# Lower halves of one gate-up chunk in eight: from a POOL transfer instead of VectorE

## The chip, the cores and the metric

One core of a Trainium2 chip runs the kernel. The metric is the time of one execution on the device in microseconds; the median of several runs is given.

## The reference

One layer of a hybrid encoder on 256 tokens with 2048 features, in float32. Two of its parts are feed-forward networks (FFN), one at the start and one at the end, with 5632 inner features:

```
def swiglu(x, w_gate_up, w_down):
    gate, up = jnp.split(x @ w_gate_up, 2, axis=-1)
    return (jax.nn.silu(gate) * up) @ w_down

ff = swiglu(rms_norm(x, pre_norm_ffn1), w_ffn1_gate_up, w_ffn1_down)
x = x + 0.5 * rms_norm(ff, post_norm_ffn1)
...  # one combined projection, HGRN2 recurrence, windowed attention, output projection
ff = swiglu(rms_norm(x, pre_norm_ffn2), w_ffn2_gate_up, w_ffn2_down)
x = x + 0.5 * rms_norm(ff, post_norm_ffn2)
```

The change is in `x @ w_gate_up`, a product of 256 x 2048 by 2048 x 11264, in both FFNs.

## The kernel before

**Numbers in two parts.** TensorE multiplies a shorter float type (`F32R`). To keep float32's accuracy each operand is taken as an upper part `h`, its rounding to that type, and a lower part `l`, the remainder `x - h`, and a product is three: `ah*h`, `ah*l`, `al*h` (`three`, each of its matmuls is on line 415). The weights are split on the way. Each half chunk of 128 x 1024 weights comes into `raw`, ScalarE copies it into `h` with the rounding (line 175), and VectorE subtracts, `l = raw - h` (line 176). `split_half` makes the two tiles, `split` and `split_load` do so for both halves of a chunk.

**Gate-up.** `Gated` works in `NG` = 11 groups (`group(g)`, g from 0 to 10), each of 512 gate columns with the 512 up columns that belong to them. A group goes over the 2048 input features in eight chunks of 256 (`order`, `work`, `pos` from 0 to 7). A chunk is 1 MB of weights, loaded in two transfers of 512 KB on SP's queue (`load`, line 151), one for each half, and one half (index k) is 128 features by 512 gate and 512 up columns. An ordinary chunk is 24 matmuls: 2 halves x 2 blocks of 128 tokens x 2 column blocks x 3, the first half's twelve ahead of the second's, and in each three the second uses `l`. The chunks at positions 2 and 4 (`sums`, `seven`) are done with seven block products instead of eight, 21 matmuls, and need four splits and some sums on VectorE first. At position 6 the seven products are folded into the four banks (`fold`, lines 477 to 485), and there, as at position 5, the products go bank by bank. After a group, `units` makes silu(gate) * up (ScalarE line 844, VectorE line 845), transposes it on TensorE (line 856) and splits it into `ht`. A group's transposes run after the next group's chunk 0.

**Buffers.** `raw` has three buffers (`rawp`, 1 MB each), `h` and `l` have five each (`hip`, `lop`, a half chunk each). A new tile waits for the last reader of the tile it takes the place of: a copy into `h` for TensorE's products on the `h` five before, a load into `raw` for the last engine that read the `raw` three before.

**Order.** Each engine runs its instructions in the order of its own list, and waits at each for the semaphores that it needs. For this part the order within an engine follows the program, moved about a little by the planner that places the instructions; it is written out by hand only at the start and at the seams between stages (`manual_schedule`). POOL's queue is used for small vectors at the start (line 116 and lines 995 to 1006), and POOL itself for a few small operations.

Of the kernel before, what the change touches and what calls it, by code (L numbers as in the profile page):

```python
# [11 lines left out]
F32 = mybir.dt.float32  # L12
F32R = mybir.dt.float32r
# [4 lines left out]
ALU = mybir.AluOpType  # L18
AX = mybir.AxisListType

P = 128
# [16 lines left out]
def hymba_layer_kernel(  # L38
# [25 lines left out]
    nc = tc.nc  # L64
# [4 lines left out]
    hip = ctx.enter_context(tc.tile_pool(name="hip", bufs=5))  # L69
    lop = ctx.enter_context(tc.tile_pool(name="lop", bufs=5))  # L70
# [5 lines left out]
    def nm(s):  # L76
        uid[0] += 1
        return f"{s}_{uid[0]}"
# [61 lines left out]
    def load(src, between=None):  # L140
        raw = rawp.tile([P, 2048], F32, tag="raw", name=nm("raw"))
        if len(src.shape) == 4:

            dst = raw.rearrange("p (a n b) -> p a n b", a=src.shape[1], n=src.shape[2])
            parts = [(dst[:, a], src[:, a]) for a in range(src.shape[1])]
        else:
            parts = [(raw.rearrange("p (a b) -> p a b", a=src.shape[1]), src)]
        for i, (to, of) in enumerate(parts):
            if i and between:
                between()  # L150
            nc.sync.dma_start(to, of)
        return raw

    def split_load(src, hp=hip, lp=lop, between=None, middle=None):
        return split(load(src, between), hp, lp, middle)

    def split(raw, hp=hip, lp=lop, middle=None):
        hs, ls = [], []
        for i in range(2):
            if i and middle:  # L160
                middle()
            h, l = split_half(raw, i, hp, lp)
            hs.append(h)
            ls.append(l)
        return hs, ls

    def split_half(raw, i, hp=hip, lp=lop):
        part = raw[:, i * 1024 : (i + 1) * 1024]
        h = hp.tile([P, 1024], F32R, tag="h", name=nm("h"))
        l = lp.tile([P, 1024], F32R, tag="l", name=nm("l"))  # L170
        split_act(h, l, part)
        return h, l

    def split_act(hi, lo, src):
        nc.scalar.copy(hi, src)  # L175
        nc.vector.tensor_tensor(lo, src, hi.bitcast(F32), ALU.subtract)  # L176
# [144 lines left out]
    class LeadN:  # L321


        def __init__(self, w, c0, slot):
            self.w, self.c0, self.slot = w, c0, slot
# [56 lines left out]
    class Blocks:  # L382
# [3 lines left out]

        def __init__(self, tiles, sums):
            self.tiles, self.sums = tiles, sums

        def begin(self, order, c=None):  # L390

            self.order, self.pos, self.seen = order, 0, {}
            self.c = c or [[pa(), pa()], [pb(), pb()]]
            self.p = None
            at = [i for i, u in enumerate(order) if u in self.sums]
            some = len(at)
            plain = len(order) - some
            self.after = at[-1] + 1 if at else len(order) - 1

            self.rest = 6 * (len(order) - self.after - 1)  # L400
            self.of = {}
            for i in range(4):
                self.of["p", i] = 3 * some
                self.of["c", i // 2, i % 2] = 6 * plain + (3 * some if i < 3 else 0)
# [25 lines left out]
        def seven(self, u):  # L430
# [9 lines left out]
                four[:, 0:2], four[:, 0::3], four[:, 1:2].to_broadcast([P, 2, 512]), ALU.add  # L440
            )
            lower = split_half(raw, 1)
            nc.vector.tensor_tensor(b22, b11, b22, ALU.add)  # L443
            upper = split_half(raw, 0)
            nc.vector.tensor_tensor(b21, b22, b21, ALU.add)  # L445
            last = split_half(raw, 1)
# [40 lines left out]
        def work(self, upto):  # L487

            while self.pos < upto:
                u = self.order[self.pos]  # L490
                if u in self.sums:
                    self.seven(u)
                else:
                    hs, ls = split_load(self.source(u))
                    if self.pos == self.after + 1:
                        self.fold()
                    places = [(k, m, n) for k in range(2) for m in range(2) for n in range(2)]
                    if self.pos in (self.after, self.after + 1):

                        places.sort(key=lambda at: at[1:])  # L500
                    for k, m, n in places:
                        self.plain(u, hs, ls, m, n, k)
                self.pos += 1
# [253 lines left out]
    class Gated(Blocks):  # L757
# [6 lines left out]

        def group(self, g, c=None):
            self.g = g
            self.begin(range(KT // 2), c)

        def source(self, u):
# [27 lines left out]
    def ffn(gated, w_dn, post_gain, again, gain=None, lead=None, aside=None):  # L797

        with ExitStack() as st:
# [96 lines left out]

            again_order = [u for u in order if u < NU - LATE] + [u for u in order if u >= NU - LATE]
            rows = Pairs(w_dn, [order, again_order], hts, sums, work, post_gain)
            rows.half_gain(far["pool"])
            rows.work(1)  # L900
# [16 lines left out]
    with tc.manual_schedule():  # L917
# [9 lines left out]
        raw = rawp.tile([P, 2048], F32, tag="raw", name=nm("raw"))  # L927
        first = gated.source(0)

        def arrive(i):  # L930
            nc.sync.dma_start(raw[:, i * 512 : (i + 1) * 512], first[:, i // 2, i % 2])

        h, l = (
            p.tile([P, 1024], F32R, tag=t, name=nm(t)) for p, t in ((hip, "h"), (lop, "l"))
        )
# [32 lines left out]
        hs, ls = zip((h, l), split_half(raw, 1))  # L968
# [519 lines left out]
```

## Time and profile before

| | |
|---|---|
| median of 3 runs | 1866.79 us (1866.19 to 1867.09) |
| the profiled execution | 1864.63 us |
| its span | 1862.9 us |
| granted TensorE clock | 0.999 |
| TensorE, VectorE, ScalarE, POOL busy | 1842.0, 1539.1, 1070.6, 33.7 us |
| DMA | 365.79 MB, mean 196 GB/s |
| first FFN's groups 1 to 10 | about 62 to 492 us, 43.06 us each |
| second FFN's groups 1 to 10 | about 1192 to 1622 us |

In the rows, PE is TensorE, PEld its weight loads, DVE is VectorE, ACT is ScalarE, POOL is GpSimd, SP issues transfers; a name with q is that engine's queue or sequencer. A row of the timeline has start, length (us), engine, line, operation, tile written <- tiles read, shape, and in brackets the idle time of the engine ahead of it with what ended it. A row of groups has count, busy time, mean length in ns, then idle time and its releasers. A busy TensorE counts its matmuls with their modelled ends, each 0.39 us long though one starts every 0.227 us.

### The profile page before, as it was taken

Reading aid. Unit: us, or ns where it says so; the run is one execution under the profiler, and the core shown is the slowest. Engines: PE = TensorE matmul, PEld = TensorE weight load, DVE = VectorE, ACT = ScalarE, POOL = GpSimd, SP = SyncE. Lnnn points to the kernel's source line nnn. Section 1 sums busy time; section 2 is a strip of 40 time slices with the busy share of each in tenths; the row PEclk is TensorE's granted clock in tenths of the full one; section 3 lists DMA queues with packets and bytes.
Section 4 is the critical chain, followed back from the end, with each engine's and each line's share of the span. In section 5 each row is a group of like instructions: output and inputs, shape, how many; then the busy total and the mean of one; then the engine's idle time right before and its main releaser. Section 6 shows DMA issues by size and latency. Waiting matters only on the chain.

```text
span 1862.9 us, 23299 instructions
## 1 busy us (share of the span) xinstructions
PE 1842.0 (99%) x8680; PEld 1534.1 (82%) x8680; DVE 1539.1 (83%) x1924; ACT 1070.6 (57%) x1429; POOL 33.7 (2%) x47
## 2 busy tenths in 40 slices
PE   8999999999999999999999999999999999999998
PEld 6888888888887887888888887888888888887886
DVE  6988888888888888567787788988888788888887
ACT  6555555555555556576677656555555555565553
POOL 1000000000000002000000001000000000000000
PEclk9999999999999999999999999999999999999999
DMA  7555565556555465655565556555665556555564
GB/s 242 190 204 198 187 205 201 181 181 202 194 209 224 178 259 193 204 181 165 169 186 148 178 190 227 186 196 182 209 208 193 202 191 204 182 192 211 186 256 161
DMA packets 180882, 365.79 MB, mean 196 GB/s; under 512 B 9256, under 2 KB 56448, under 8 KB 180000
## 3 DMA queue, kind: packets, MB, share of 16 engines
q1 hardware_dynamic: 180416, 364.17, 57.1%
q8 instruction: 68, 1.11, 0.3%
q14 instruction: 46, 0.38, 0.1%
q0 software_dynamic: 352, 0.14, 0.0%
HBM read 360.06 MB, written 4.21 MB: 196 GB/s over the span
## 4 chain that ended last, share of the span: by engine, by line
PE 77%; DVE 15%; ACT 3%; issue 3%; DMA 0%; POOL 0%; ACTq 0%; DVEq 0%; SPq 0%; POOLq 0%
PE pa L415 30%; PE pb L415 28%; DVE l L176 9%; PE pa L298 8%; PE pa L303 4%; ACT h L175 2%; DVE raw L439 2%; DVE raw L445 1%; DVE raw L443 1%; DVE sp L176 1%; PE pa L349 1%; PE pa L348 1%; PE pa L347 1%; ACT xt L226 1%; PE pa L856 0%
## 5 line engine op out<-in xcount | busy, mean ns | idle before, releaser
L175 ACT CAST h<-raw 128x1024 fp32r<-128x1024 f32 (+1 forms) x825 | 808.9, 1010 | 670.7 <-PE pb L415 300.6
L176 DVE TENSOR_TENSOR l<-raw,h 128x1024 fp32r<-128x1024 f32 (+1 forms) x825 | 936.2, 1166 | 242.4 <-ACT h L175 209.4
L415 PE MATMUL pa<-h,xt 128*128 128x512 f32 x1248 | 431.4, 392 | 1.4 <-ACT h L175 1.4
L415 PE MATMUL pb<-h,xt 128*128 128x512 f32 x1168 | 407.5, 390 | 0.5 <-ACT xt L226 0.5
L415 PEld LDWEIGHTS pa<-h,xt 128*128 128x128 f32 x1248 | 234.6, 188 | 50.2 <-ACT h L175 2.4
L415 PEld LDWEIGHTS pb<-h,xt 128*128 128x128 f32 x1168 | 219.2, 188 | 46.2 <-ACT xt L226 0.7
L415 PE MATMUL pa<-l,xt 128*128 128x512 f32 x624 | 243.8, 391 | 2.1 <-DVE l L176 2.0
L415 PE MATMUL pb<-l,xt 128*128 128x512 f32 x584 | 227.2, 389 | 0.0
L415 PE MATMUL pa<-h,ht 128*128 128x512 f32 x560 | 193.4, 390 | 0.0
L415 PE MATMUL pb<-h,ht 128*128 128x512 f32 x488 | 171.9, 390 | 0.2 <-DVE pb L483 0.2
L298 PE MATMUL pa<-xt,h 128*128 128x512 f32 x672 | 164.7, 394 | 0.0
L298 PEld LDWEIGHTS pa<-xt,h 128*128 128x128 f32 x672 | 123.0, 188 | 23.6
L415 PEld LDWEIGHTS pa<-l,xt 128*128 128x128 f32 x624 | 117.4, 188 | 27.2 <-DVE l L176 4.0
L415 PEld LDWEIGHTS pb<-l,xt 128*128 128x128 f32 x584 | 109.7, 188 | 22.5
L415 PEld LDWEIGHTS pa<-h,ht 128*128 128x128 f32 x560 | 105.1, 188 | 22.5 <-DVE pa L482 0.5
L415 PE MATMUL pa<-l,ht 128*128 128x512 f32 x280 | 109.3, 390 | 0.0
L415 PEld LDWEIGHTS pb<-h,ht 128*128 128x128 f32 x488 | 91.6, 188 | 19.9 <-DVE pb L483 0.8
L439 DVE TENSOR_TENSOR raw<-raw 128x1024 f32<-128x1024 f32 x80 | 97.8, 1222 | 1.7
L415 PE MATMUL pb<-l,ht 128*128 128x512 f32 x244 | 95.0, 389 | 0.0
L303 PE MATMUL pa<-xt,l 128*128 128x256 f32 x672 | 91.5, 285 | 0.0
L303 PEld LDWEIGHTS pa<-xt,l 128*128 128x128 f32 x672 | 87.1, 191 | 3.2
L415 PEld LDWEIGHTS pa<-l,ht 128*128 128x128 f32 x280 | 52.6, 188 | 11.5 <-DVE l L176 0.7
(270 smaller groups left out, 2011.9 us busy)
## 6 DMA issues: line engine op xcount, KB each, us to landing
raw<-in_w_ffn_gate_up_dram SPq DMA_DIRECT2D x350, 512.0 KB, 4.8
raw<-in_w_ffn_down_dram SPq DMA_DIRECT2D x88, 1024.0 KB, 5.1
raw<-in_w_mix_in_dram SPq DMA_DIRECT2D x52, 1024.0 KB, 5.0
raw<-in_w_mix_out_dram SPq DMA_DIRECT2D x16, 1024.0 KB, 5.0
pg<-in_post_norm_ffn_dram SPq DMA_DIRECT2D x4, 512.0 KB, 5.9
X<-in_x_dram SPq DMA_DIRECT2D x2, 1024.0 KB, 5.9
bias<-row SPq DMA_DIRECT2D x16, 128.0 KB, 4.5
kept<-X SPq DMA_DIRECT2D x2, 1024.0 KB, 4.7
```

The source lines that it names most:

```text
L175: nc.scalar.copy(hi, src)
L176: nc.vector.tensor_tensor(lo, src, hi.bitcast(F32), ALU.subtract)
L226: last["act"] = nc.scalar.mul(hi, src, g)
L298: nc.tensor.matmul(slot[f], weights(hs, kk, f), xcol(xt, k), start=(k == 0), stop=(k == KT - 1))
L303: nc.tensor.matmul(slot[f][:, 0:T], weights(ls, kk, f), xcol(xt, kh * 8 + kk, 0), start=False, stop=False,)
L347: nc.tensor.matmul(dst, xh, h[:, o : o + n], start=(k == 0), stop=False)
L348: nc.tensor.matmul(dst, xh, l[:, o : o + n], start=False, stop=False)
L349: nc.tensor.matmul(dst, xl, h[:, o : o + n], start=False, stop=(k == KT - 1))
L415: nc.tensor.matmul(self.bank(at), lhs, rhs, start=(n == 1), stop=n in (ends, self.of[at]), skip_group_check=n > ends,)
L439: nc.vector.tensor_tensor(four[:, 0:2], four[:, 0::3], four[:, 1:2].to_broadcast([P, 2, 512]), ALU.add)
L443: nc.vector.tensor_tensor(b22, b11, b22, ALU.add)
L445: nc.vector.tensor_tensor(b21, b22, b21, ALU.add)
```

## The change

The chunk at position 0 in the groups 1 to 10 of each FFN (20 chunks, 40 halves) gets its lower parts in another way. ScalarE writes `h` as before, and then `-h` into `l`; a transfer on POOL's queue then reads the same weights from HBM once more and adds them to what lies in `l`. VectorE has no part in these halves, and `raw` is read by ScalarE alone. The chunks at positions 1 to 7, group 0 and the rest of the kernel stay.

```
+    def split_by_dma(raw, src):
+        hs, ls = [], []
+        for i in range(2):
+            part = raw[:, i * 1024 : (i + 1) * 1024]
+            h = hip.tile([P, 1024], F32R, tag="h", name=nm("h"))
+            l = lop.tile([P, 1024], F32R, tag="l", name=nm("l"))
+            nc.scalar.copy(h, part)
+            nc.scalar.mul(l, h.bitcast(F32), -1.0)
+            nc.gpsimd.dma_start(l.rearrange("p (n c) -> p n c", n=2), src[:, i], accum_op=ALU.add)
+            hs.append(h)
+            ls.append(l)
+        return hs, ls
...
@@ class Blocks, __init__
             self.tiles, self.sums = tiles, sums
+            self.by_dma = ()
...
@@ class Blocks, work
-                    hs, ls = split_load(self.source(u))
+                    if self.pos in self.by_dma:
+                        hs, ls = split_by_dma(load(self.source(u)), self.source(u))
+                    else:
+                        hs, ls = split_load(self.source(u))
...
@@ class Gated, group
             self.g = g
+            self.by_dma = (0,) if g else ()
             self.begin(range(KT // 2), c)
```

## Prediction

> **What bounds the kernel now.** I read the page's header and busy shares, then busy time by stretches of the gate-up groups, then the timeline around one group's start, then the DMA rows.
>
> ```profile
> span 1862.9 us, 23299 instructions
> PE 1842.0 (99%) x8680; PEld 1534.1 (82%) x8680; DVE 1539.1 (83%) x1924; ACT 1070.6 (57%) x1429; POOL 33.7 (2%) x47
> ...
> PE 77%; DVE 15%; ACT 3%; issue 3%; DMA 0%; POOL 0%; ACTq 0%; DVEq 0%; SPq 0%; POOLq 0%
> ```
>
> TensorE is busy almost throughout, yet the chain that ended last runs for 15% through VectorE, so one has to ask in which stage. The change touches only gate-up groups 1 to 10 of each FFN. These are the stretches that hold them, and one group by itself; the columns are length, then busy time and instructions of each engine, granted TensorE clock, DMA share, GB/s:
>
> ```profile
> core 0: us, PE busy (x) PEld busy (x) DVE busy (x) ACT busy (x) POOL busy (x), PEclk, DMA share, GB/s
> 62.00:505.00 443.00, 443.00 (x1999) 367.61 (x1999) 372.70 (x428) 239.65 (x275) 0.00 (x0) 1.00 0.59 198
> 1192.00:1622.00 430.00, 430.00 (x1939) 357.07 (x1938) 358.25 (x410) 229.25 (x260) 0.00 (x0) 1.00 0.58 196
> 153.09:196.15 43.06, 43.06 (x196) 35.76 (x195) 35.78 (x42) 23.01 (x26) 0.00 (x0) 1.00 0.58 196
> ```
>
> TensorE is busy 443.00 of 443.00 us and 430.00 of 430.00 us, at a granted clock of 1.00. A group takes 43.06 us. VectorE is busy for 35.8 us of it and idle for 7, so it never ends a wait of TensorE here. The 15% of VectorE in the chain lies elsewhere: TensorE's idle time is 1862.9 - 1842.0 = 20.9 us, and none of it is in these stretches.
>
> **The change part by part.**
>
> *Removed from VectorE.* Two subtractions for each of 20 groups (10 in each of two FFNs), 40 in all, and added to ScalarE, 40 negations of the same shape, which I price like its copies:
>
> ```profile
> L176 DVE TENSOR_TENSOR l<-raw,h 128x1024 fp32r<-128x1024 f32 x743 | 887.3, 1220 | 239.9 <-ACT h L175 207.0 <-PE pa L303 29.7
> L175 ACT CAST h<-raw 128x1024 fp32r<-128x1024 f32 x743 | 763.5, 1054 | 665.7 <-PE pb L415 297.3 <-DVE raw L445 136.2 <-DVE raw L439 98.5
> ```
>
> That is 40 x 1.22 = 48.8 us of VectorE off, and 40 x 1.05 = 42 us of ScalarE on (2.1 us for each group, 23.0 to 25.1 of 43.06). VectorE's share is worth nothing: TensorE has no gap that it could close. ScalarE's is covered by its 20 us of idle time in a group, as long as nothing behind the negations is due at once. So the whole question is whether the new way to the lower part is still ahead of TensorE. Here is the start of the group whose first product runs at 191.27 (start, length, engine, line, tiles):
>
> ```profile
> 179.91 2.00 ACT L175 CAST h<-raw 128x1024 fp32r<-128x1024 f32 x2 [3.11 <-PE pb L415]
> 185.80 2.01 ACT L175 CAST h<-raw 128x1024 fp32r<-128x1024 f32 x2 [3.89 <-PE pb L415]
> 188.75 1.05 ACT L175 CAST h<-raw 128x1024 fp32r<-128x1024 f32 x1 [0.94 <-PE pb L415]
> 189.71 0.68 ACT L844 ACTIVATE z<-pa,scales 128x512 f32<-128x512 f32 x1
> ...
> 182.77 1.21 DVE L176 TENSOR_TENSOR l<-raw,h 128x1024 fp32r<-128x1024 f32 x1
> ...
> 186.89 2.36 DVE L176 TENSOR_TENSOR l<-raw,h 128x1024 fp32r<-128x1024 f32 x2 [2.30 <-ACT h L175]
> ...
> 191.27 0.39 PE L415 MATMUL pa<-h,xt 128*128 128x512 f32 x1
> 191.50 0.39 PE L415 MATMUL pa<-l,xt 128*128 128x512 f32 x1
> ...
> 193.99 0.39 PE L415 MATMUL pa<-h,xt 128*128 128x512 f32 x1
> 194.22 0.39 PE L415 MATMUL pa<-l,xt 128*128 128x512 f32 x1
> ```
>
> There are five `h` and five `l` buffers, so a half's copy waits until TensorE has done with the half five before it. Counting halves back from 191.27, the second copy at 179.91 is the first half of the group's first chunk, and the first copy at 185.80 is its second half; both are released by TensorE, at a fixed distance ahead of their use. This lead, not VectorE, is what the new chain has to live in:
>
> - First half: the copy ends at 181.92, the negation in the slot after it at 182.9; its `l` is due at 191.50. Room: 8.6 us.
> - Second half: copy and negation fill the slot 185.80 to 187.81; `l` is due at 194.22. Room: 6.4 us. Before, VectorE had it at 188.1, six microseconds early.
>
> The negations push the next chunk's copies and the `z` at 189.71 by some 0.3 us; that chunk is due only a whole chunk (24 products) after 191.27, so this is nothing.
>
> *Added to the POOL queue.* 40 transfers of 512 KB, each read from HBM a second time and added onto what lies in `l`. No accumulating transfer is in this trace, so its landing must be bounded by the nearest rows.
>
> ```profile
> q1 hardware_dynamic: 180416, 364.17, 57.1%
> ...
> row<-bias_rows POOLq DMA_DIRECT2D x1, 16.0 KB, 1.8
> ...
> DMA packets 32, 0.02 MB, mean 4 GB/s; under 512 B 24, under 2 KB 24, under 8 KB 32
> ...
> bias_rows<-in_onehot_dram POOLq DMA_DIRECT2D x1, 64.0 KB, 4.7
> ...
> GB/s 369 379 399 379 389 379 389 369 307 328 328 389 379 287 307 287 379 399 420 461 287 256 236 113 103 10 10 0 0 0 0 0 0 0 0 0 0 0 0 72
> ...
> 182.90:191.50 8.60, 8.60 (x40) 7.12 (x38) 5.71 (x6) 4.33 (x5) 0.00 (x0) 1.00 0.59 182
> 187.90:194.22 6.32, 6.32 (x30) 5.23 (x28) 5.70 (x7) 2.95 (x4) 0.00 (x0) 1.00 0.73 233
> ```
>
> The loads' packets (2 KB) take 0.571 x 16 x 1862.9 us / 180416 = 94 ns of an engine. A 512 KB transfer is 256 such runs, 16 for each of 16 engines. On quiet engines (the packets row: 54 to 58 us, 4 GB/s) a POOL transfer with at most one such packet an engine landed in 1.8 us; with two packets an engine, under loads at 370 to 400 GB/s (the GB/s row is the stretch 24 to 32 us, in forty slices), 4.7 us. An accumulating packet has to read its destination as well as its source; I take 2 x 94 = 188 ns.
>
> - Quiet end: 1.8 + 15 x 0.188 = 4.6 us.
> - Contended end, a load's packet between any two: 4.7 + 14 x (0.188 + 0.094) = 8.6 us.
>
> The engines are 0.59 busy in the first half's room and 0.73 in the second's. The load that fills the buffer which chunk 0 leaves is issued when VectorE has finished the second half; now ScalarE alone frees it, some 1.3 us earlier, which moves load out of the late stretch into the early one, so I take the mean, 0.66, for the second half: 4.6 + 0.66 x 4.0 = 7.3 us against 6.4 of room, **0.9 us late**. The first half, 4.6 + 0.59 x 4.0 = 7.0 us against 8.6, is in time. TensorE takes its products in order and has nothing to spare, so a late `l` moves everything behind it: 20 x 0.9 = 17 us, the sum.
>
> The Trainium skill's "Collectives: The Full Stack", section "The bandwidth ceiling: the fold count and why AG ≠ RS ≠ AR", says of another kind of adding transfer that the addition costs no time of its own but reads two sources over one read side, which halves its rate. By it the packet would be 188 ns too; no run here shows it yet.
>
> *Other queues.* POOL's engine is idle in these groups, so a transfer waits behind nothing there, with one exception: in the first FFN the write of `row` waits for VectorE until 55.15 us, and three periods of 43.06 before 182.9 is 53.7, so group 1's first transfer may stand 1.4 us behind it, within its 1.6 us to spare.
>
> ```profile
> 55.15 0.55 POOL L1006 DMA_DIRECT2D row<-bias_rows  x1 [11.34 <-DVE s L379]
> ...
> SPq L151 <- DVE l L176: 1355.7, 309, 14.2
> ...
> 188.14 0.54 SPq L151 DMA_DIRECT2D raw<-in_w_ffn_gate_up_dram  x1
> ...
> DMA to landing us min/median/max: 3.9/4.9/10.6
> ```
>
> SP's loads wait mostly for VectorE to free `raw` (the second row); for chunk 0 that wait gets shorter. They will share engines with 1 MB more in a group that moves 8 (20 groups: 21 MB). The load at 188.14 goes into the buffer that chunk 0 left, so with three buffers it is chunk 3, three chunks of 24 or 21 products after 191.27: a load that lands 3 us late stays hidden. A negation frees nothing early and keeps `l` no longer.
>
> **The sum against the median.** The profiled execution took 1864.63 us, of which 1862.9 is span; with 17 us it would be 1882. The median of the three runs shown is 2.2 us above it, so 1866.8 + 17 = 1884 us.
>
> **The rivals.**
>
> *The transfer lands in time* (the other side: no change). If a packet costs 94 ns, because reading the destination runs beside reading the source, the ends are 1.8 + 15 x 0.094 = 3.2 and 4.7 + 14 x 0.188 = 7.3 us, at 0.66 together 5.9 us: inside the 6.4, and the time stays at 1866.8. It decides at about 128 ns a packet. For it: the margins are small, and the profile's groups have no other wait. Against it: two thirds of the room are spent under loads. The Trainium skill's "DMA: Bandwidth & Descriptors", section "Anatomy of one DMA — SWDGE (gpsimd) path", gives 2.0 us and bytes by 436 GB/s for a POOL transfer: an estimate of 3.2 us here, the same as my quiet end, and by that rule alone nothing would be late.
>
> *The transfer is much slower.* If the write back costs a third pass, a packet is 282 ns: 6.0 and 10.0 us, at 0.66 8.6 us, 2.2 us late, 44 us in all: 1911 us. The slowest load in this trace landed after 10.6 us (last row above); such a landing would be 4.2 us late, 84 us in all: 1951 us. The first half would then be late too, by 2.0 us, but inside the same shift.
>
> *Faster.* VectorE's 48.8 us would have to be on the path. It would need TensorE to wait in these groups, and it does not; what is left is a different order of instructions at the seams between stages, out of the 20.9 us of idle time there. I give it a price of 5 us (an estimate: a quarter of that idle time): 1862 us.
>
> **How the numbers follow.** A change under 0.2% (3.7 us, 0.19 us a group) can't be told from none here. Late by 0.2 to 1.6 us: 0.40, the forecast, 1871 to 1899 by itself. In time: 0.38. Much slower: 0.17. Faster: 0.05. So slower 0.57, same 0.38, faster 0.05. The range must reach the case of no change, and to 1920 on the upper side (2.7 us late), which leaves out a part of the slow rival.
>
> **What the profile after would show.** TensorE's idle time in 62 to 505 us rises from zero, in one gap a group, ahead of the first product on `l` of the second half, ended by a DMA on POOL's queue; the group grows from 43.06 to about 43.9 us; POOL's transfers land after about 7 us; VectorE is busy some 33.4 us in a group, ScalarE 25.1. With no gap and 43.06 us, the packet was cheap. The prediction is wrong in kind if the gap stands at the first half, if loads of `raw` come late instead, or if TensorE's order in the first chunk is another, so that the due times above no longer hold.

## The result

| | before | after |
|---|---|---|
| median of the runs taken side by side (4 each) | 1866.49 us | 1972.14 us |
| lowest to highest | 1866.01 to 1867.09 | 1964.52 to 1978.07 |
| profiled execution, span | 1864.63, 1862.9 us | 1968.82, 1966.6 us |

The ratio is 1.0559, 95% interval 1.053 to 1.0588: 105.7 us slower. The forecast was 1884 us with a range to 1920. The direction and the place were right, the size was six times too small.

The new function moves line numbers: copy, negation and transfer of the changed chunk are L181, L182 and L183; L175, L176 and L415 of before are L189, L190 and L430. The page's header, busy shares and chain, and two rows of its groups:

```profile
span 1966.6 us, 23493 instructions
PE 1882.6 (96%) x8680; PEld 1554.7 (79%) x8680; DVE 1496.8 (76%) x1884; ACT 1110.7 (56%) x1469; POOL 77.6 (4%) x87
...
q1 hardware_dynamic: 180416, 364.17, 53.5%
q0 software_dynamic: 11232, 21.11, 6.3%
...
PE 23%; DVE 7%; DMA 4%; issue 2%; ACT 1%; DVEq 0%; ACTq 0%; POOL 0%; POOLq 0%
...
l<-in_w_ffn_gate_up_dram POOLq DMA_DIRECT2D x40, 512.0 KB, 8.5
```

VectorE is 42 us less busy (1539.1 to 1496.8, 40 instructions fewer), ScalarE 40 us more. DMA, which had 0% of the chain, has 4%. TensorE's idle time is now 1966.6 - 1882.6 = 84 us against 20.9. The waits of TensorE name what ended them (us in total, times, longest):

```profile
PE pa L430 <- DMA l<-in_w_ffn_gate_up_dram: 63.2, 25, 7.3
```

By stretch of time, after (length, busy time and instructions, then granted clock, DMA share, GB/s; the second row is one group, with all engines):

```profile
62.00:505.00 443.00, 410.38 (x1769) 0.96 0.65 201
153.09:200.88 47.79, 44.92 (x196) 36.53 (x195) 33.55 (x40) 24.99 (x28) 2.16 (x2) 0.96 0.64 196
```

The groups were gapless at a clock of 1.00; now TensorE is idle for 7% of the stretch, and the clock itself is lower. One group takes 47.79 us, not 43.06. Inside it, TensorE's timeline (start, length) and the granted clock in three stretches of 3.4 us:

```profile
164.58 0.39 PE L430 MATMUL pa<-h,xt 128*128 128x512 f32 x1
165.16 0.47 PE L430 MATMUL pa<-l,xt 128*128 128x512 f32 x1 [0.19 <-DMA l<-in_w_ffn_gate_up_dram]
...
167.78 0.39 PE L430 MATMUL pa<-h,xt 128*128 128x512 f32 x1
170.85 0.77 PE L430 MATMUL pa<-l,xt 128*128 128x512 f32 x1 [2.68 <-DMA l<-in_w_ffn_gate_up_dram]
```

```profile
166.90:170.30 3.40, 1.27 (x6) 1.00 1.07 295
170.30:173.70 3.40, 2.85 (x7) 0.50 0.32 122
173.70:177.10 3.40, 3.40 (x21) 1.00 0.00 0
```

Products follow one another every 0.227 us. The first half's `l` product, due at 164.81, is 0.35 us late; the second half's, due at 168.01, starts at 170.85, 2.84 us late. Then comes the part that nobody had on the list: for the next 3.4 us TensorE runs at half its clock, and its products come every 0.43 us. The trace has 19 such stretches in the groups, each with one of the 20 long waits: 18 of 3.41 us and, with the longest wait, one of 10.24. From the starts of all products (40 to 1855 us), against before: waits 74.6 - 7.0 = 68 us, halved clock 30 us, wider spacing 2 us. That is 100 of the 104 us between the two profiled executions; the other 4 lie outside this count.

The Trainium skill's "TensorE: Matmul & The Clock Gate", section "Part 1: The HAM clock gate (the "warmup" mystery)", gives a free-running window of 3413 ns and a half clock after an idle one. The length agrees (18 of 3.41 us, one of three times that). The condition does not: the window ahead of the slow one above was not idle, TensorE was busy for 1.27 of its 3.40 us.

What the trace shows instead is a matter of windows. The starts of the halved stretches lie whole multiples of 3.413 us apart (122.51, 170.30 and 218.09 are 14 each), so these windows can be laid over the whole trace. In after, the windows right ahead of the halved stretches have a TensorE busy for 0.15 to 1.36 us; every other window of the groups at full clock has 1.8 us or more. So it counts where a wait falls, and not its length alone: the one long wait that no halved stretch follows (its product starts at 1590.82, 2.3 us late) lies across the edge of two windows, which keep 1.82 and 2.84 us. The other runs put the line between some 1.5 and 1.8 us.

### The profile page after: what moved, and what is told of

The parts are those of the page before. It is cut to its first block, busy times and chain, and to the rows that moved or that the text cites. A ratio compares the mean times of both kernels' runs of the same rounds, so it can differ in the third digit from the quotient of the medians.

```text
span 1966.6 us, 23493 instructions
## 1 busy us (share of the span) xinstructions
PE 1882.6 (96%) x8680; PEld 1554.7 (79%) x8680; DVE 1496.8 (76%) x1884; ACT 1110.7 (56%) x1469; POOL 77.6 (4%) x87
## 3 DMA queue, kind: packets, MB, share of 16 engines
q0 software_dynamic: 11232, 21.11, 6.3%
## 5 line engine op out<-in xcount | busy, mean ns | idle before, releaser
L190 DVE TENSOR_TENSOR l<-raw,h 128x1024 fp32r<-128x1024 f32 (+1 forms) x785 | 889.8, 1165 | 383.4 <-ACT h L189 351.2
L189 ACT CAST h<-raw 128x1024 fp32r<-128x1024 f32 (+1 forms) x785 | 770.5, 1008 | 691.8 <-PE pb L430 334.7
L430 PE MATMUL pa<-h,xt 128*128 128x512 f32 x1248 | 443.3, 402 | 1.4 <-ACT h L189 1.4
L430 PE MATMUL pb<-h,xt 128*128 128x512 f32 x1168 | 415.7, 400 | 0.5 <-ACT xt L240 0.5
L430 PE MATMUL pa<-l,xt 128*128 128x512 f32 x624 | 254.1, 407 | 65.8 <-DMA l<-in_w_ffn_gate_up_dram 63.2
L430 PEld LDWEIGHTS pa<-h,xt 128*128 128x128 f32 x1248 | 240.8, 193 | 51.2 <-ACT h L189 2.4
L430 PEld LDWEIGHTS pb<-h,xt 128*128 128x128 f32 x1168 | 227.3, 195 | 50.5 <-ACT xt L240 0.9
L430 PE MATMUL pb<-l,xt 128*128 128x512 f32 x584 | 233.5, 400 | 0.0
L430 PEld LDWEIGHTS pa<-l,xt 128*128 128x128 f32 x624 | 120.7, 193 | 102.5 <-issue 69.3
L430 PE MATMUL pa<-h,ht 128*128 128x512 f32 x560 | 193.5, 390 | 0.0
L430 PE MATMUL pb<-h,ht 128*128 128x512 f32 x488 | 171.8, 390 | 0.0
L430 PEld LDWEIGHTS pb<-l,xt 128*128 128x128 f32 x584 | 114.0, 195 | 24.5
L430 PEld LDWEIGHTS pa<-h,ht 128*128 128x128 f32 x560 | 105.1, 188 | 22.6 <-DVE pa L497 0.6
L430 PE MATMUL pa<-l,ht 128*128 128x512 f32 x280 | 109.3, 390 | 0.0
L430 PEld LDWEIGHTS pb<-h,ht 128*128 128x128 f32 x488 | 91.6, 188 | 19.6 <-DVE pb L498 0.4
L430 PE MATMUL pb<-l,ht 128*128 128x512 f32 x244 | 95.0, 389 | 0.0
L183 POOL DMA_DIRECT2D l<-in_w_ffn_gate_up_dram x40 | 43.8, 1105 | 848.7 <-ACT l L182 750.1
```

What stands on the lines that cost most here:

```text
L183: nc.gpsimd.dma_start(l.rearrange("p (n c) -> p n c", n=2), src[:, i], accum_op=ALU.add)
L430: nc.tensor.matmul(self.bank(at), lhs, rhs, start=(n == 1), stop=n in (ends, self.of[at]), skip_group_check=n > ends,)
```

## The experiments

The letters in the expectations: A was my explanation at that point, the others its rivals, as each text says; P and N belong to the last five. All ratios are to before, run beside the kernel.

### Is it the addition, or the transfer at all?

`plain` sends the same bytes to the same place without adding (so `l` holds the weights, not their lower part):

```
-            nc.gpsimd.dma_start(l.rearrange(...), src[:, i], accum_op=ALU.add)
+            nc.gpsimd.dma_start(l.rearrange(...), src[:, i])
```

> The same 40 transfers on POOL's queue without the addition (l then holds the weights themselves, so the sum is left out; the products take as long). Theory A, the second half's transfer lands some 8.7 us after it is issued, made of a start behind the loads in flight, 16 packets of 178 ns an engine, and a tail, and the wait of 2.5 to 3 us then halves the clock for one 3.4 us stretch: without the addition a packet is 84 ns, so 1.5 us less: landing about 7.2 us, a wait of 1.3 us, too short to halve the clock, 20 x (1.3 + 0) = 26 us over the kernel before, about 1893. Rival B, the addition alone makes it late: landing under 6 us, no wait, 1867. Rival C, the queueing behind the loads is all and the packets' price nothing: landing still 8.5 us, about 1970.

1890.62 us, 1.0132 (1.0113 to 1.015). Its landing and its waits, from the page's DMA issues and the waits of TensorE:

```profile
l<-in_w_ffn_gate_up_dram POOLq DMA_DIRECT2D x40, 512.0 KB, 6.0
```

```profile
PE pa L430 <- DMA l<-in_w_ffn_gate_up_dram: 15.5, 16, 4.9
```

2.5 us of the landing and 82 us of the time belong to the addition; 24 us would be lost with a plain copy too. That the time came out near the 1893 expected is luck in part: the landing was 6.0 us, not 7.2, and instead of 1.3 us in each group there were 7.2 us of waits in the two first groups and short ones elsewhere.

`quiet` is the kernel before with transfers of this size put one behind another at its end, where no weight load runs (three plain, three adding, on POOL's queue; three plain ones on SP's queue behind them landed after 3.9 to 5.2 us). Its time, 1884.63 us in one run, has the chain in it and says nothing else:

> The kernel before with transfers of 512 KB added at its end, each waiting for the one before, when no load runs: three times a plain one and an adding one on POOL's queue, then three plain ones on SP's. Theory A (8.7 us in the changed kernel = start behind the loads in flight + 16 packets of 178 ns + a tail in which a few engines are behind later loads): alone the adding transfer lands in about 5.5 us, of which 2.85 us are packets, and the plain one 1.5 us sooner, about 4. Rival B (the addition itself is slow): the adding one takes 8 us alone too. The time of the whole kernel is longer by the chain, some 40 us, and says nothing.

POOL's timeline (L1420 plain, L1421 adding; the bracket is the wait for the one before to land):

```profile
1839.46 1.13 POOL L1421 DMA_DIRECT2D probe_l<-in_w_ffn_gate_up_dram  x1 [6.21 <-DMA probe_l<-in_w_ffn_gate_up_dram]
1845.70 0.73 POOL L1420 DMA_DIRECT2D probe_l<-in_w_ffn_gate_up_dram  x1 [5.12 <-DMA probe_l<-in_w_ffn_gate_up_dram]
1850.09 1.08 POOL L1421 DMA_DIRECT2D probe_l<-in_w_ffn_gate_up_dram  x1 [3.65 <-DMA probe_l<-in_w_ffn_gate_up_dram]
1856.19 0.73 POOL L1420 DMA_DIRECT2D probe_l<-in_w_ffn_gate_up_dram  x1 [5.03 <-DMA probe_l<-in_w_ffn_gate_up_dram]
1860.97 1.08 POOL L1421 DMA_DIRECT2D probe_l<-in_w_ffn_gate_up_dram  x1 [4.04 <-DMA probe_l<-in_w_ffn_gate_up_dram]
```

From one start to the next an adding transfer takes 6.24 and 6.10 us, a plain one 4.39 and 4.78 (landed after 5.7 to 6.0 and 4.1). The first plain one, ahead of these rows, still ran beside the last loads and took 6.7 us. The prediction's quiet end of 4.6 us was too low by more than a microsecond; the room was 6.4.

### What the waits bring with them

`fill12` puts twelve products of no use (0.227 us each, 2.7 us) just ahead of the second half's products, the second of which is the late one:

```
+                        if self.pos in self.by_dma and (k, m, n) == (1, 0, 0):
+                            spare.append(pa())
+                            for i in range(12):
+                                nc.tensor.matmul(spare[0], ..., hs[0][:, 0:512], ...)
```

> Twelve products of no use (2.7 us) go ahead of the second half of chunk 0 in TensorE's order, into a bank that the transposes then overwrite; the wait is filled, nothing else moves. Theory A, the halved clock comes from TensorE's idling in the wait: the clock stays whole, 19 x 1.7 = 32 us less, about 1940. Rival C, the clock (or TensorE) is slowed by the transfer itself: the clock still halves and the time stays near 1972.

1951.78 us, 1.0457 (1.0436 to 1.0478). 20 x 12 x 0.227 = 54 us of work were added, and the kernel is 20 us faster than after. Two halved stretches are left of 19 (6.83 and 3.41 us), both in first groups, and the clock is back (0.980 in after):

```profile
core 0: 1945.3 us, clock 0.996
```

So the halved clock is a consequence of the waits, with a price of its own (30 us in after, 3.3 here), and not a state of the chip. The expectation was 12 us too low: waits of 15.3 us are left.

### Order on ScalarE

The timelines of ScalarE and POOL in after, for the group shown above:

```profile
154.17 1.05 ACT L181 CAST h<-raw 128x1024 fp32r<-128x1024 f32 x1
155.26 1.06 ACT L182 ACTIVATE l<-h 128x1024 fp32r<-128x1024 f32 x1
158.66 1.05 ACT L181 CAST h<-raw 128x1024 fp32r<-128x1024 f32 x1 [2.34 <-PE pb L430]
159.61 1.05 ACT L189 CAST h<-raw 128x1024 fp32r<-128x1024 f32 x1
160.56 1.05 ACT L182 ACTIVATE l<-h 128x1024 fp32r<-128x1024 f32 x1
```

```profile
156.68 1.07 POOL L183 DMA_DIRECT2D l<-in_w_ffn_gate_up_dram  x1 [40.66 <-ACT l L182]
161.97 1.08 POOL L183 DMA_DIRECT2D l<-in_w_ffn_gate_up_dram  x1 [4.22 <-DVE l L190]
```

The second transfer's bracket names VectorE, but both start 0.36 us behind the end of their negation. The next chunk's copy (L189) stands between the second half's copy and its negation: 0.95 us. `negfirst` holds it back:

```
+                    elif self.by_dma and self.pos == 1:
+                        with tc.issue_after(last["neg"].ins):
+                            hs, ls = split_load(self.source(u))
```

> The copies of the next chunk are held behind the second half's negation, so the transfer is issued one ScalarE slot (0.95 us) sooner. Theory A: the wait at the second half falls from 2.8 to about 1.9 us, and where that is too short to halve the clock the group gains another 1.7 us: between 1972 - 19 = 1953 and 1972 - 19 - 33 = 1920. Rival D, the transfer only queues behind the load that SP issued 2 us ahead of it, so it starts when that load's data is through whatever the time of issue: same landing, 1970.

1956.48 us, 1.0483 (1.0451 to 1.0515): 16 us better than after, beyond the end of what was expected. The negation did move up, but the transfer that starts earlier lands later after its start (median of the second halves 9.1 for 8.6), and most of the wait stays (after's row: 63.2, 25 times); 13 halved stretches are left:

```profile
PE pa L430 <- DMA l<-in_w_ffn_gate_up_dram: 53.6, 26, 4.0
```

### One half at a time

`first_half` and `second_half` leave the other half to VectorE:

```
+            if i != 0:    # first_half; second_half: i != 1
+                h, l = split_half(raw, i)
+                ...
+                continue
```

> Only the first half of chunk 0 comes by the adding transfer, the second half's lower part from VectorE as before. Theory A: room 8.2 us from its issue, landing 8.3 as in the changed kernel, because the load of chunk 2 stands ahead of it: waits of 0.3 to 0.5 us in half of the groups and of 2 to 5 us in the first group of each FFN, no halved clock otherwise: 1872 to 1885. The first prediction's sum (landing 7.0): no wait, 1867. Rival C (transfers slow TensorE as such): half of the loss, 1920.

> Only the second half of chunk 0 comes by the adding transfer. Theory A: landing over 8 us against 6 of room, a wait of about 2.5 us in each group and the halved clock behind it: 20 x (2.5 + 1.7) = 84 us, 1935 to 1955. Rival G, it is the two transfers together that make the second late: landing under 6.5 us, 1867 to 1880.

1881.96 us, 1.0083 (1.0068 to 1.0098), and 1889.8 us, 1.0129 (1.0114 to 1.0144). With the first half alone the steady groups have one wait of 0.3 us (6.5 us fall into the first group of each FFN, with 4 us of halved clock behind them). With the second alone there are 17 waits, 15.9 us in all, most of them under 1 us, the longest 2.8. Second half alone, POOL and TensorE:

```profile
147.96 1.07 POOL L188 DMA_DIRECT2D l<-in_w_ffn_gate_up_dram  x1 [42.93 <-DVE l L195]
```

```profile
152.89 0.39 PE L435 MATMUL pa<-h,xt 128*128 128x512 f32 x1
153.87 0.47 PE L435 MATMUL pa<-l,xt 128*128 128x512 f32 x1 [0.59 <-DMA l<-in_w_ffn_gate_up_dram]
```

The product was due at 153.12, 5.16 us behind the transfer's start, not 6.4. The transfer landed after 5.78 us, as quickly as on quiet engines, and was still late. I had expected a landing over 8 us and 1935 to 1955: a miss. Rival G, that it takes both transfers to make the second one land late, had the landing right (under 6.5) and the time too low (to 1880), since the room is shorter than 6.4. The two halves are not independent: their sum (15 + 23 us) is far from 106. Together they make the second half late (median landing 8.6 for 5.8; the first half's is 8.0 for 7.8), and the wait gets long enough to halve the clock.

The same run shows that the length of a wait does not decide on the clock. A wait of 1.84 us (to 1518.71) lies within one window, the first row; the next window is at half clock. A wait of 2.80 us (to 1610.43) lies across two, the third and fourth row; the one behind them is at full clock:

```profile
1516.75:1520.16 3.41, 1.57 (x7) 1.23 (x7) 2.33 (x3) 0.98 (x1) 0.00 (x0) 1.00 0.84 299
1520.16:1523.57 3.41, 3.41 (x12) 2.80 (x11) 0.28 (x1) 0.98 (x1) 0.00 (x0) 0.50 0.03 10
1605.50:1608.91 3.41, 2.13 (x10) 1.43 (x8) 2.35 (x4) 1.04 (x1) 0.00 (x0) 1.00 1.08 242
1608.91:1612.32 3.41, 1.89 (x8) 1.61 (x9) 2.21 (x3) 0.00 (x0) 0.00 (x0) 1.00 0.69 261
1612.32:1615.73 3.41, 3.41 (x20) 2.89 (x19) 1.37 (x2) 2.02 (x3) 0.00 (x0) 1.00 0.00 0
```

`second_negfirst` adds the edit of `negfirst` to it, which should have bought the missing microsecond:

> Only the second half by the adding transfer from HBM, in groups 1 to 10, with the negation right behind its copy. Theory A: the transfer lands in 5.8 us as it did without that order, its room grows from 5.1 to 6.1 us, so the waits of 0.7 us in each group go: from 1890 to between 1868 and 1875, what is left being group 1. Rival J, the landing moves with the time of issue (it queues behind a load): the waits stay, 1885 to 1890.

1902.1 us, 1.019 (1.0172 to 1.0207): a miss, and to the wrong side, 12 us above rival J's range too. This run shows how the queues share the engines. DMA queues (packets, MB, share of the 16 engines; q1 carries the loads, q0 POOL's transfers) of `second_negfirst` in 150 to 153 and 153 to 156 us, its transfer having started at 149.92:

```profile
q1 hardware_dynamic: 463, 0.92, 97.0%
...
q0 software_dynamic: 220, 0.44, 89.3%
q1 hardware_dynamic: 87, 0.15, 15.8%
```

And of after in 157 to 160, 160 to 163, 163 to 166 and 166 to 169 us, with transfers started at 156.68 and 161.97:

```profile
q1 hardware_dynamic: 413, 0.81, 86.8%
...
q0 software_dynamic: 200, 0.41, 80.6%
q1 hardware_dynamic: 124, 0.22, 22.5%
...
q1 hardware_dynamic: 495, 0.97, 84.0%
q0 software_dynamic: 75, 0.12, 22.6%
...
q0 software_dynamic: 256, 0.50, 90.6%
q1 hardware_dynamic: 121, 0.22, 20.6%
```

The queues do not alternate packet by packet. A transfer's packets run together, behind those of a load that was there first, and the next load runs behind them. So what a transfer costs in landing depends on the load ahead of it. SP's queue issued two loads shortly ahead of each transfer; here are the medians over the groups, in us from the transfer's start:

| transfer | the two loads were issued | they land | it lands |
|---|---|---|---|
| after, first half | 1.15 and 0.56 before | 2.9 and 4.9 | 8.0 |
| after, second half | 2.29 and 1.70 before | 4.1 and 6.3 | 8.6 |
| `second_half` | 2.29 and 1.71 before | 1.8 and 3.1 | 5.8 |
| `second_negfirst` | 1.48 and 0.89 before | 2.6 and 4.0 | 7.0 |

Where the loads are through after 4 us or more, the transfer lands 2.3 to 3.1 us behind the second of them. In after the second half's loads stand themselves behind the first half's transfer, and so they land later than the same loads in `second_half`. In `second_negfirst` the transfer moved up by 0.8 us towards loads that stayed where they were, and landed 1.2 us later after its start: the mechanism of rival J, at a higher price. (Why it loses 0.4 us by it, and does not come out even, stays open.)

The Trainium skill's "DMA: Bandwidth & Descriptors", section "Queues, rings and completion order", says that an engine takes turns between queues by whole packets of some 9 to 17 descriptors; one engine's share of a transfer here is 16 runs of 2 KB (each a packet in the rows; I take it for a descriptor there), so by that rule whole transfers would take turns. The rows above agree.

### Taking the load out of the way

`fromraw` reads the weights from `raw`, where they still lie, instead of from HBM. That also keeps `raw` from being loaded again until the transfers have landed, so two things change at once:

```
-            nc.gpsimd.dma_start(l.rearrange(...), src[:, i], accum_op=ALU.add)
+            nc.gpsimd.dma_start(l, part, accum_op=ALU.add)
```

> The addition takes the weights from raw, on the chip, not from HBM a second time; raw is then held until the transfer has landed, so the load that takes its place is issued after it and no longer stands ahead of the second half's transfer. Theory A: without that load ahead the second half's transfer starts at once, its landing falls from 8.7 to some 5.5 us, no wait at the second half; the first half's still stands behind the load of chunk 2 and stays 0.3 us late: 1867 to 1875. Rival B, the adding packets' price decides: landing stays over 8 us and the time over 1950. Rival E, holding raw longer makes the loads late: the wait moves to ScalarE's copies, 1880 to 1950.

1873.98 us, 1.0041 (1.0027 to 1.0056). From group 2 on second halves land after 4.8 to 5.3 us; 4.0 us of waits are left, in the first groups. `fromraw_g2` leaves group 1 out (`g > 1`):

> The transfer adds raw from the chip, in groups 2 to 10 of each FFN alone (18 chunks instead of 20). Theory A: in those groups both halves landed in time before, the 8 us that were left were group 1's, where the planner puts a copy that waits for a load ahead of both negations; and VectorE's freed time (18 x 2 x 1.22 = 44 us) is worth nothing: 1866, within 0.2% of the kernel before. Rival H, VectorE's time is worth something once nothing is late: below 1862. Rival I, more DMA work costs by itself: 1870 or more.

1867.86 us, 1.0007 (0.9998 to 1.0015): no wait for a transfer, and the groups are gapless again:

```profile
62.00:505.00 443.00, 443.00 (x1999) 1.00 0.70 220
```

This is the direct answer on VectorE: 36 of the 40 subtractions are off it, nothing is late, and the time is that of before.

`hold` separates the two: it reads from HBM, and a one-column instruction on POOL that reads `raw` and the second `l` keeps the next load waiting until the transfers have landed:

```
+        held = stat.tile([P, 1], F32, tag="held", name=nm("held"), bufs=1)
+        nc.gpsimd.tensor_tensor(held, raw[:, 0:1], ls[1].bitcast(F32)[:, 0:1], ALU.add)
```

> The weights come from HBM as in the changed kernel, but a one-column addition on POOL reads raw and the second half's l once that transfer has landed, so raw is held and the load that takes its place is issued after the landing. Theory A, what made the second half late was that load, issued 2 us ahead of the transfer: the second half lands in 5 to 5.5 us without a wait, 1870 to 1885, close to the kernel with raw as the source. Rival F, it was the second reading from HBM: landing stays over 8 us, near 1970.

> The adding transfer from HBM in groups 2 to 10, with three things mended: the negation stands right behind its copy, raw is held until the second half has landed, group 1 is left out. Theory A, the second half's 5.7 us landing against a room of 5.1 us from the transfer's start becomes 5.7 against 6.1, the first half's 7.9 against 8.2: no waits, 1866 to 1870. The alternative, that the first half's landing at its slowest (8.7) still ends late: 1870 to 1876. Rival F (the second reading from HBM costs as such): over 1880.

`hold`: 1896.51 us, 1.0157 (1.014 to 1.0174). `hold_neg_g2` (with the edit of `negfirst`, from group 2): 1881.45 us, 1.0069 (1.0054 to 1.0085). Both missed, though TensorE's waits had nearly gone: 7.5 us in `hold` and 1.4 us in `hold_neg_g2`. The loss stood where no such transfer runs. Products of the down stage of the first FFN (528 to 738 us; busy us, mean ns of one), first before, then `hold_neg_g2`:

```profile
L415 PE MATMUL pa<-h,ht 128*128 128x512 f32 x238 | 82.0, 390 | 0.0
```

```profile
L432 PE MATMUL pa<-h,ht 128*128 128x512 f32 x247 | 86.4, 395 | 0.0
```

By their starts they follow one another every 232 ns instead of 227, without a wait, at a granted clock of 1.00. What can reach so far is the extra tile: it shifts what lies behind it in the core's memory. `shifted4` is before with the spare tile ahead of that memory four bytes wider, every instruction the same:

```
-    stat.tile([P, 104], F32, tag="line", name="line", bufs=1)
+    stat.tile([P, 105], F32, tag="line", name="line", bufs=1)
```

> The kernel before with one edit: the spare tile ahead of most of the core's memory is 105 columns wide instead of 104, so that what lies behind it moves by 4 bytes; every engine's list of instructions is the same as before's. Theory P (place): the two versions with a held load lost their time because their extra tile of 4 bytes moved the operands of TensorE. In their profiles its products follow one another 232 ns apart in the down stages, 227 ns in before, and 227.8 for 226.7 ns in the gate-up groups, without a wait. Then this kernel takes 1878 to 1886 us, with the same spacings. Theory N (no effect of place; the loss comes from the held loads): 1866 to 1868 us, 227 ns.

1875.73 us, 1.0048 (1.0036 to 1.0061), 2 us under the expected range, with the same widening in the same place:

```profile
L415 PE MATMUL pa<-h,ht 128*128 128x512 f32 x241 | 84.3, 395 | 0.0
```

The next two took four bytes out of the spare tile:

> The version with the load held and the next copies behind the second negation, in groups 2 to 10 alone, but the spare tile is 103 columns wide, so that the extra tile of 4 bytes moves nothing behind it. Under theory P its time is that of a kernel without waits: 1866 to 1870 us (before 1866.5 plus at most the 1.1 us of waits that its predecessor's profile shows and 1.5 us of group 2), spacing 227 ns in the down stages; then adding from HBM costs nothing where the load behind it is held and nothing else stands between. Under theory N it stays at 1881 us.

> The version with the load held alone (all groups, instructions in the order of after), the spare tile 103 columns wide. Under theory P the 15 us outside the waits go: 1896.5 - 15 = 1881 us, of which 7.5 us are waits by its predecessor's profile, a part of them in the first group of each projection, 4 us of halved clock at most. Under theory N it stays at 1896 us.

1880.51 and 1896.22 us (1.0073 and 1.0155): no change, as theory N had it. But the addresses in the compiled program show that a tile's room is rounded up to 32 bytes: 105 columns had moved everything by 32, and 103 had taken nothing out. The weights' `raw`, `h` and `l` lie ahead of the spare tile and never moved; `ht`, the other operand of the down stage's products, did. With 96 columns it lies where before has it:

> As the version with the load held and the next copies behind the second negation (groups 2 to 10), with the spare tile 96 columns wide. shifted4's four bytes, which the allocation rounds up to 32, cost 9 us by the verdict and widened the spacing to 232 ns in the down stages; 103 columns had taken 4 bytes out, which the rounding gave back, so all behind the extra tile still lay 32 bytes off. 96 columns take out the 32: every operand of the projections lies where before has it. Theory P: spacing 227 ns in the down stages, 1866 to 1871 us (before's 1866.5 to 1867.9, plus the 1.5 us of waits that its predecessor's profile shows). If the held load or the transfer costs more than its waits: 1873 us or more (1880.5 minus the 8 us of the displacement), with the spacing back at 227 ns.

> As the version with the load held alone (all groups), with the spare tile 96 columns wide. Theory P: 1896.2 less the displacement's 8 to 11 us, 1885 to 1888 us: what is left are the waits, 18 - 7 = 11 us by the spacing of the products of its predecessor's profile, and 3 us of halved clock. If the displacement isn't the cause: 1896 us.

1870.36 us, 1.0019 (1.0009 to 1.003), and 1886.58 us, 1.0102 (1.0087 to 1.0117): both as theory P had it. In `hold_neg_g2_line96` the spacing is back, and the second halves, read from HBM, are nearly all in time (down stage, groups, waits, and a second half's transfer with the instruction on POOL that waits for it):

```profile
L432 PE MATMUL pa<-h,ht 128*128 128x512 f32 x244 | 84.1, 390 | 0.0
```

```profile
62.00:505.00 443.00, 441.46 (x1991) 1.00 0.71 219
```

```profile
PE pa L432 <- DMA l<-in_w_ffn_gate_up_dram: 2.2, 4, 0.9
```

```profile
104.12 1.10 POOL L183 DMA_DIRECT2D l<-in_w_ffn_gate_up_dram  x1 [3.34 <-ACT l L182]
110.23 0.39 POOL L187 TENSOR_TENSOR held<-raw,l 128x1 f32<-128x1 f32 x1 [5.01 <-DMA l<-in_w_ffn_gate_up_dram]
```

The transfer lands 6.0 us after its start. So, with `ht` back in its place, three things together turn 106 us into some 3.5: the next load held back, the negation straight behind its copy, and the change kept out of group 1. The load held back alone leaves 19 (`hold_line96`); the other two were not run apart. That also rules out rival F, the second reading from HBM, into whose range `hold_neg_g2` had come. None of the versions is faster than before.

## Why the prediction was wrong

**VectorE's time is worth nothing: right.** `fromraw_g2` shows it by itself (1.0007).

**Where and what waits: right.** One long gap a group, ahead of the second half's first `l` product, ended by a DMA on POOL's queue, with the first half nearly in time (0.35 us), is what the section on the profile after named. VectorE's 33.55 and ScalarE's 24.99 us in a group are the 33.4 and 25.1 forecast.

**The packet: right.** q0's share gives 0.063 x 16 x 1966.6 / 11232 = 176 ns against 188 (the 2 KB packets alone, without some small ones: 190). The rival with a third pass (282 ns) came nearer to the time, for a wrong reason.

**The landing: this is the step that failed.** The prediction put 7.3 us between a quiet end of 4.6 and a contended end of 8.6, by weighing them with the share of time in which the engines are busy (0.66). Two of the three did not hold. The quiet end is 5.7 to 6.0 (`quiet`). And a share is no weight where queues take turns by whole transfers: one either finds a load ahead of it and waits for all of it, or doesn't. The median of the second halves is 8.6 us, 1.3 above the forecast; the contended end had that size, but by packets in between and not by a load ahead. In the group shown it took 8.74 us (161.97 to 170.71). In that group loads were ahead both times (q1 in 157 to 160 and in 163 to 166 us). The load that `hold` keeps back is the one into chunk 0's own buffer, and with it the late landings go: the prediction saw that this load comes earlier ("issued ... some 1.3 us earlier") and took it to lower the share.

**Room and ends.** "Copy and negation fill the slot" failed for the second half: the next chunk's copy took the place behind the copy (0.95 us). In the group shown the copy itself came 9.35 us ahead of its use, 8.42 in before, so that the room from the negation's end was again 6.40 us; in `second_half`, where it came 8.41 ahead, it was 5.5. Not priced were 0.36 us from the negation to POOL's start and 0.14 from landing to product. So 0.9 forecast + 1.4 landing + 0.36 + 0.14 = 2.8 us, the gap measured.

**A late product only moves what is behind it: wrong.** "20 x 0.9" had no term for the clock. At 0.9 us a group none would have been due: such a wait leaves a window 2.5 of its 3.41 us, and none with 1.8 or more was followed by a halved one. At 2.8 us and more it adds 30 us to 68 us of waits.

**Group 1.** The 1.6 us to spare behind the write of `row` were not the limit. By ScalarE's timeline a copy that waits for its load is in line ahead of both negations there, and TensorE waited 7.4 us in the first FFN and 4.3 in the second; leaving the group out took 6 us off `fromraw`.

## What to carry to other kernels

Where TensorE has no gap, work taken off another engine buys nothing, and the one question about the new way is whether its last step still lands ahead of use; take its start as the last of everything in line ahead of it on its engine, the next tile's work too. Price a transfer that shares engines with a stream of large loads as landing behind a whole load, not at a mean, and look at which buffer your own edit frees just ahead of it. Take it that a wait which leaves TensorE idle for most of a 3.41 us window costs some half as much again, and that an extra small tile is a change by itself.

## What the hardware showed that I had not expected

- TensorE's clock went by windows of 3.413 us on one grid. In after, a window with TensorE busy for 1.36 us or less was followed by one at half clock, one with 1.8 us or more never; the length of the wait did not decide (`second_half`: halved after 1.84 us within one window, not after 2.80 us across two). Together that cost 30 us, some 1.6 us for each of the 19 stretches.
- Moving `ht` and all else behind the spare tile by 32 bytes, with every instruction unchanged, cost 0.48% (0.36 to 0.61%): products of the down stages 232 ns apart instead of 227, at a granted clock of 1.00. Of these products' operands only `ht` moved; other tiles moved too, and none was moved by itself.
- A 512 KB transfer that adds takes 1.6 to 1.9 us longer than a plain one on quiet engines (5.7 to 6.0 against 4.1 us landed), and 2.5 us longer beside the loads (8.5 against 6.0).
